# A hybrid encoder block: seven half-size products for the first half of K only, plain products for the second

## The chip, the cores and the metric

The kernel runs on one core of a Trainium2 chip. The metric is device time in microseconds (us) of one launch; the median of three runs of the kernel before is 1590.06 us (1582.69 to 1591.21). The engines are named as the profile names them: PE is TensorE (PEld its weight loads), DVE is VectorE, ACT is ScalarE, POOL is GpSimd, SP is SyncE, which issues nearly all DMAs; ACT issues some too.

## The reference

One layer on x of 1024 tokens by 2048 features, all in float32:

```python
h = rmsnorm(x, norm_w[l])
proj = jnp.einsum('bsd,de->bse', h, w_in[l])                 # 2048 -> 5632
q_a, k_a, v_a, g_a, q_r, k_r, v_r, g_r = jnp.split(proj, points, axis=-1)
attn = windowed_attention(q_a, k_a, v_a, attn_sink[l], rel_bias)      # 16 heads of 64, +-128 tokens
attn = rmsnorm(attn, attn_out_norm_w[l]) * jax.nn.silu(g_a)
ret = bidirectional_retention(rotary(q_r), rotary(k_r) * 64 ** -0.5, v_r, decay_fwd, decay_bwd)
ret = head_groupnorm(ret, ret_gn_w[l]) * jax.nn.silu(g_r)             # 8 heads, chunks of 128
mixed = jnp.concatenate([attn, ret], axis=-1)
x = x + jnp.einsum('bse,ed->bsd', mixed, w_out[l])           # 2048 -> 2048
return rmsnorm(x, final_norm_w)
```

(The reshapes into heads are left out here.)

## The kernel before

**Precision.** Every float32 operand of the large products is split into a high and a low fp32r part: ACT casts the high part (`split`, L163), POOL or DVE subtracts it to get the low part (L157). A product is then three matmuls: high by high, high by low, low by high. `wh` and `wl` are the parts of a weight tile, `hT` holds 28 rows of 128x1024: in one row the high part of a 128x512 block of activations and beside it the low part.

**Stages.** K is the 2048 features, sixteen tiles of 128.

1. Six plain units (`STD`: keys, values and queries of the attention), each 256 columns by 1024 tokens over all of K, four PSUM banks a unit. Meanwhile `combine(0)` and `combine(1)` make, for each half of K, 28 blocks of sums and differences of the normalised activations and store them in `cd`.
2. Sixteen units (`FAST`: the gates `ga` and `gr`, the retention's `qk` and `vr`), each 256 columns by 1024 tokens, twice: q = 0 to 15 is the first half of K, q = 16 to 31 the second. Each time the unit is a 2x2 by 2x2 block product done with seven half-size products instead of eight (`multiply`, L1001 to L1003; four K tiles and so 12 matmuls a product, 84 a unit). The seven weight tiles are sums and differences that `prep_sums` makes, on POOL in the first half of K and on DVE in the second, each split before use. `collect` puts the results together on ACT and DVE. The first half goes to DRAM (`yd`); the second half loads it back into the tiles `e11`, `e12`, `e2` (`partial`, L1027), adds its own, and passes the unit on: SiLU for the gates (stored in `gd`), rotation for `qk` (`rqk`), transposes for `vr` (L1106, stored in `vrd` by ACT's queue, L107).
3. The output projection: two halves of 512 tokens, four units of 512 columns each, sixteen K rows a unit (L1309 to L1311), weights split by ACT and DVE. The last unit is done bank by bank with weights that lie ready (L1335 to L1337).

**What runs between.** After every third large matmul the code calls `point()`, which advances three queues of generators: `jobs` (attention while the first half of K runs; retention while the second half does, one head pair p at a time, a step each 2.42 points), `post`, and `aux`. A retention job loads keys, queries and values (`rk`, `rq`, `vt`, L665 to L667) and starts multiplying by `vt` at its fifth step (L707). `premix` in `aux` (L845 to L847) loads an attention row `md`, its gate `gd` and the norm `rbd`, multiplies them on POOL and stores the row back to `md`; later `mixed_load` (L863) and `mixed_rows` load each row again and split it into `hT` on ACT (L878) and DVE (L160). For the first 512 tokens they do that at the very end of the second half of K and in the first output unit, in the order `ROWS`; for the last 512 tokens in the output units after it.

**Order.** Each engine works through its instructions in the order in which they stand. The order is set by where the code records them and by the generators' paces. Short-lived 128x512 tiles (`t2`) come from a ring of six: the seventh waits until the first is free. The raw weight tiles (`r`) have eight buffers, `wh` and `wl` three each, and the large products four PSUM banks (`psMa` and `psMb`, two each).

## Time and profile before

| what | us |
|---|---|
| profiled execution, device time | 1581.0 |
| its span, first to last instruction | 1579.2 |
| plain units, to 301 | 301 |
| first half of K, 301 to 730 | 429 |
| second half of K, 730 to 1195 | 465 |
| output, first 512 tokens, 1195 to 1392 | 197 |
| output, last 512 tokens, 1392 to the end | 187 |
| median of the three runs | 1590.06 |

The stage borders are the starts of the stage's first large matmul in the trace. In a group line of the profile the last fields are busy time, mean duration of one in ns, idle time of the engine just before, and what ended that idle time. A matmul's recorded duration is longer than the distance to the next one, because matmuls overlap; the distance is what counts. PEclk is the share of the TensorE clock that was granted.

### The profile page before, as it was taken

To read this page: it belongs to the slowest core of one execution; us is meant where nothing else is said; L and a number is where in the kernel's file an instruction comes from. 1 tells how busy PE (TensorE), PEld (TensorE's weight loads), DVE (VectorE), ACT (ScalarE), POOL (GpSimd) and SP (SyncE) were. 2 spreads that over 40 slices of the span, in tenths; PEclk is the share of its full clock that TensorE was granted. 3 is DMA by queue.
4 is the path that set the end of the run, shared out by engine and by line. 5 is a ranking of instruction groups with operands and counts; after the bars stand their busy time and mean duration, and the time that the engine had idled before them with its cause. 6 is when DMAs were issued, how large, how long until landed. Compare 5 with 4: busy or idle time off the path is not lost.

```text
span 1579.2 us, 21950 instructions
## 1 busy us (share of the span) xinstructions
PE 1486.1 (94%) x7250; PEld 1230.2 (78%) x7250; DVE 912.4 (58%) x1872; ACT 666.0 (42%) x1401; POOL 614.3 (39%) x481
## 2 busy tenths in 40 slices
PE   8999999999999999999998989799888989999997
PEld 6898877778888888887777777677676868878886
DVE  6565345863653664577758868659684353364323
ACT  5311135765765775775321332232343343324210
POOL 3232221356557456544653635665443200113000
PEclk9999999999999999999999999899998999999999
DMA  8888768784564564538763554684737864565403
GB/s 311 286 268 299 259 180 288 246 271 128 148 185 134 160 181 142 167 118 295 238 226 136 187 187 150 209 288 135 244 136 238 279 217 131 161 216 196 128 20 107
DMA packets 195406, 311.73 MB, mean 197 GB/s; under 512 B 29355, under 2 KB 67243, under 8 KB 194652
## 3 DMA queue, kind: packets, MB, share of 16 engines
q1 hardware_dynamic: 164828, 289.36, 56.4%
q10 hardware_dynamic: 30464, 20.98, 4.2%
q8 instruction: 57, 0.93, 0.2%
q14 instruction: 57, 0.47, 0.1%
HBM read 216.38 MB, written 93.88 MB: 196 GB/s over the span
## 4 chain that ended last, share of the span: by engine, by line
PE 50%; DMA 17%; DVE 10%; issue 9%; POOL 7%; ACT 4%; SPq 3%; POOLq 0%; ACTq 0%; DVEq 0%
POOL wl L157 4%; PE psMa L1003 4%; PE psMa L1001 4%; PE psMa L1002 4%; PE psMb L1001 3%; PE psMb L1003 3%; PE psMb L1002 3%; PE psST L574 2%; DMA t<-mpd 2%; PE psST L1310 2%; PE psMa L1310 2%; PE psST L1309 2%; DMA cd<-crow 2%; PE psST L1311 2%; DVE t L157 2%
## 5 line engine op out<-in xcount | busy, mean ns | idle before, releaser
L157 POOL TENSOR_TENSOR wl<-r,wh 128x512 fp32r<-128x512 f32 x224 | 299.4, 1340 | 328.1 <-ACT wh L163 296.6
L1001 PE MATMUL psMa<-hT,wh 128*128 128x512 f32 x512 | 209.8, 410 | 15.0 <-DVE bmv L757 6.5
L1003 PE MATMUL psMa<-hT,wl 128*128 128x512 f32 x512 | 205.0, 400 | 6.5 <-POOL wl L157 6.5
L1002 PE MATMUL psMa<-hT,wh 128*128 128x512 f32 x512 | 202.9, 396 | 0.0
L163 ACT CAST wh<-r 128x512 fp32r<-128x512 f32 x224 | 136.8, 617 | 153.4 <-PE psMa L1002 67.5
L163 ACT CAST wh<-e 128x512 fp32r<-128x512 f32 x160 | 98.2, 618 | 215.7 <-PE psMb L1311 79.5
L157 DVE TENSOR_TENSOR wl<-e,wh 128x512 fp32r<-128x512 f32 x112 | 85.6, 770 | 137.0 <-ACT wh L163 134.7
L1001 PE MATMUL psMb<-hT,wh 128*128 128x512 f32 x384 | 156.5, 408 | 3.8 <-DVE bmv L757 3.8
L1003 PE MATMUL psMb<-hT,wl 128*128 128x512 f32 x384 | 152.6, 397 | 2.9 <-POOL wl L157 2.9
L157 POOL TENSOR_TENSOR wl<-e,wh 128x512 fp32r<-128x512 f32 x48 | 72.4, 1512 | 204.6 <-ACT wh L163 192.9
L1002 PE MATMUL psMb<-hT,wh 128*128 128x512 f32 x384 | 151.2, 394 | 0.0
L1001 PEld LDWEIGHTS psMa<-hT,wh 128*128 128x128 f32 x512 | 97.9, 191 | 35.1 <-issue 11.8
L1003 PEld LDWEIGHTS psMa<-hT,wl 128*128 128x128 f32 x512 | 97.7, 191 | 34.3 <-POOL wl L157 13.3
L1002 PEld LDWEIGHTS psMa<-hT,wh 128*128 128x128 f32 x512 | 98.3, 192 | 16.0
L600 DVE CUSTOM_DVE_ANT_0 P<-psST,bias,nsink 128x384 f32<-128x384 f32 (+1 forms) x128 | 74.4, 581 | 34.3 <-PE psST L592 33.3
L604 ACT ACTIVATE P<-P,nmx 128x385 f32<-128x385 f32 (+1 forms) x128 | 75.8, 592 | 37.7 <-DVE nmx L600 36.1
L1003 PEld LDWEIGHTS psMb<-hT,wl 128*128 128x128 f32 x384 | 72.9, 190 | 22.7 <-POOL wl L157 6.5
L157 POOL TENSOR_TENSOR r<-r,r 128x512 f32<-128x512 f32 x64 | 84.7, 1334 | 3.8
L1001 PEld LDWEIGHTS psMb<-hT,wh 128*128 128x128 f32 x384 | 73.2, 191 | 16.4 <-ACT wh L163 4.3
L1002 PEld LDWEIGHTS psMb<-hT,wh 128*128 128x128 f32 x384 | 73.2, 191 | 12.1
L157 DVE TENSOR_TENSOR r<-r,r 128x512 f32<-128x512 f32 x64 | 60.1, 952 | 35.7 <-POOL wl L157 34.1
L157 POOL TENSOR_TENSOR hT<-t,hT 128x512 fp32r<-128x512 f32 x16 | 21.4, 1335 | 130.7 <-ACT hT L163 130.7
(338 smaller groups left out, 3589.0 us busy)
## 6 DMA issues: line engine op xcount, KB each, us to landing
r<-in_w_fast SPq DMA_DIRECT2D x128, 256.0 KB, 3.3
e<-in_w_out SPq DMA_DIRECT2D x112, 256.0 KB, 3.4
yd<-e SPq DMA_DIRECT2D x64, 256.0 KB, 3.1
e<-yd SPq DMA_DIRECT2D x64, 256.0 KB, 3.1
t<-in_xT SPq DMA_DIRECT2D x31, 512.0 KB, 6.3
t<-cd SPq DMA_DIRECT2D x56, 256.0 KB, 4.3
e<-in_w_in SPq DMA_DIRECT2D x48, 256.0 KB, 4.6
md<-t SPq DMA_DIRECT2D x48, 256.0 KB, 2.7
```

The lines of the kernel that those rows point to most:

```text
L157: eng.tensor_tensor(o, x, y, op)
L163: A.copy(o_hi, x)
L574: T.transpose(p[:, 128 * i : 128 * i + 128], x[:, 128 * i : 128 * i + 128], ident)
L600: V.tensor_tensor_reduce(x[:, :W], p[:, :W], bias[2 * pr + c][:, k0 : k0 + W], -1.0, nsink[:, head : head + 1], ALU.add, ALU.min, nmx[:, c ...
L604: A.activation(x[:, : W + 1], x[:, : W + 1], AF.Exp, bias=nmx[:, c : c + 1], scale=-1.0, accum_out=sums[:, c : c + 1])
L1001: T.matmul(bank, wh[:, ws], hh, start=(j == 0 and p in (0, 1, 3)), stop=False, skip_group_check=True)
L1002: T.matmul(bank, wh[:, ws], hl, start=False, stop=False, skip_group_check=True)
L1003: T.matmul(bank, wl[:, ws], hh, start=False, stop=(j == 3), skip_group_check=True)
L1309: T.matmul(p, mh, wh, start=(k == 0), stop=False)
L1310: T.matmul(p, mh, wl, start=False, stop=False)
L1311: T.matmul(p, ml, wh, start=False, stop=(k == NK - 1))
```

## The change

- `prep_sums`, `multiply` and `collect` now run for the first half of K alone (16 units of 84 matmuls). `combine` makes 28 blocks instead of 56; `normalise_rest` stores the sixteen normalised blocks of the second half of K in `xd` (8 K tiles, two token halves).
- The second half is sixteen plain units. Each has four weight tiles (`w_half`, 128x512: two K tiles by 256 columns). For each tile the four PSUM banks (two column groups by two token halves) are taken one after the other, six matmuls each (two K tiles by three parts, L1310 to L1312): 96 matmuls a unit. All sixteen units use the same four banks. The part from the first half of K is loaded at the second weight tile, and DVE adds it as it empties the bank.
- What follows a unit is now a generator in `post`: `gate_post`, `rope_post`, `value_post`. The retention is let go when `value_post` has ended, two points after its last store.
- `premix`, `mixed_load` and `mixed_rows` are gone. `mixed_row` loads a row, for attention also gate and norm, multiplies on POOL, splits into `hT` on ACT and DVE, and stores nothing. The generator `mixer` makes the rows of the first 512 tokens while the plain units run, as soon as their gate or retention is done, then those of the last 512 tokens. `ROWS` has another order.
- Paces: attention 2.62 instead of 2.65 points a step, retention 2.9 instead of 2.42, `aux` 1.1 instead of 1.3 in the output.

```diff
-ROWS = [0, 1, 2, 3, 8, 9, 10, 11, 12, 13, 4, 5, 14, 15, 6, 7]
+ROWS = [0, 1, 8, 9, 2, 3, 10, 11, 12, 13, 4, 5, 14, 15, 6, 7]
...
     def w_load(i):
         if i < n_w[0] and i not in wraw and i not in wsp:
-            r = et_("e11" if i < W_STD else ("e11", "e2", "e12", "e2", "e11", "e12", "e2")[(i - W_STD) % 7])
+            if i < W_STD:
+                r = et_("e11")
+            elif i < W_ALL:
+                r = rt(F32)
+            else:
+                r = et_(("e11", "e2", "e12", "e2", "e11", "e12", "e2")[(i - W_ALL) % 7])
             SP.dma_start(r, w_src(i))
             wraw[i] = r
...
-    pt, due, pace, adue, apace = [0], [0], [2.65], [0], [2.0]
+    pt, due, pace, adue, apace = [0], [0], [2.62], [0], [2.0]
...
+    def normalise_rest():
+        loaded = {}
+        for i in range(8 + 2):
+            if i < 8:
+                loaded[i] = t4()
+                SP.dma_start(loaded[i], a["xT"][8 + i])
+            yield
+            if i >= 2:
+                x = loaded.pop(i - 2)
+                for z in range(2):
+                    y = x[:, 512 * z : 512 * z + 512]
+                    stt(V, y, y, nw[:, 6 + i : 7 + i], rb[z], ALU.mult, ALU.mult)
+                    store(xd[2 * (i - 2) + z], y, x)
+                yield
...
+    def mixed_row(kk, hf):
         sl = slice(512 * hf, 512 * hf + 512)
-        r, g, n = t2(), t2(), t2()
+        r = t2()
         SP.dma_start(r, md[128 * kk : 128 * kk + 128, sl])
-        SP.dma_start(g, gd[128 * kk : 128 * kk + 128, sl])
-        SP.dma_start(n, rbd[:, sl])
-        for _ in range(5):
-            yield
-        tt(G, g, g, n, ALU.mult)
-        tt(G, r, r, g, ALU.mult)
-        yield
-        store(md[128 * kk : 128 * kk + 128, sl], r, r, lambda: done.add(("pre", kk, hf)))
-        yield
...
+        if kk < 8:
+            g, n = t2(), t2()
+            SP.dma_start(g, gd[128 * kk : 128 * kk + 128, sl])
+            SP.dma_start(n, rbd[:, sl])
+            for _ in range(5):
+                yield
+            tt(G, g, g, n, ALU.mult)
+            tt(G, r, r, g, ALU.mult)
+        for _ in range(3):
+            yield
+        if hf and kk >= 12:
+            omix[kk] = (rt(F32R), rt(F32R))
+        c = ew[:, kk : kk + 1]
+        A.activation(orow(kk, hf, 0), r, AF.Copy, scale=c)
+        yield
+        stt(V, orow(kk, hf, 1), r, c, orow(kk, hf, 0).bitcast(F32), ALU.mult, ALU.subtract)
+        done.add(("mix", kk, hf))
+        yield
...
-        eng = V if q >= NF else G
+        eng = G
...
+    def value_post(i, tiles):
+        yield
+        yield
+        for b, t in enumerate(tiles):
+            et, hf = b // 2, b % 2
+            p = pT()
+            for c in range(4):
+                T.transpose(p[:, 128 * c : 128 * c + 128], t[:, 128 * c : 128 * c + 128], ident)
+            o = t2()
+            A.copy(o, p)
+            store_now(vrd[i, :, 4 * hf : 4 * hf + 4, 128 * et : 128 * et + 128], o.rearrange("p (c e) -> p c e", c=4))
+            yield
+            yield
+        done.add(("vr", i))
...
+    def mixer():
+        for hf in range(2):
+            order = ROWS if hf == 0 else range(16)
+            for n in range(0, 16, 2):
+                pair = order[n : n + 2]
+                need = ("ga", pair[0] // 2) if pair[0] < 8 else ("ret", (pair[0] - 8) // 2)
+                yield ready(need)
...
+    for u, (kind, i) in enumerate(FAST):
+        if u == 2:
...
-            pace[0], apace[0] = 2.42, 2.2
+            pace[0], apace[0] = 2.9, 2.2
             for g in range(4):
                 jobs.append((retention(g), None))
...
+            aux.append((mixer(), None))
+        whole = pM()
+        tiles = []
+        for w in range(4):
+            wi = W_STD + 4 * u + w
...
+            w_load(wi + 2)
+            wh, wl = wsp.pop(wi)
+            for b in range(4):
+                et, hf = b // 2, b % 2
+                p = whole[b]
+                if w == 1:
+                    tiles.append(quarter(b))
+                    SP.dma_start(tiles[b], yd[u, b])
+                for kk in range(2):
+                    ws = slice(256 * kk + 128 * et, 256 * kk + 128 * et + 128)
+                    row = 2 * (2 * w + kk) + hf
+                    hh, hl = hT[:, row, 0:512], hT[:, row, 512:1024]
+                    last = (w, kk) == (3, 1)
+                    T.matmul(p, wh[:, ws], hh, start=(w, kk) == (0, 0), stop=False)
+                    T.matmul(p, wh[:, ws], hl, start=False, stop=False)
+                    T.matmul(p, wl[:, ws], hh, start=False, stop=last)
+                    if last:
+                        tt(V, tiles[b], p, tiles[b], ALU.add)
+                    point()
+                if b == 0:
+                    w_split(wi + 1)
...
                 if un == 0:
-                    mixed_rows()
-                    if k in (5, 6, 7, 8, 9, 10):
-                        mixed_load(ROWS[k + 5], 0)
-                    if k == 13:
-                        mixed_flush()
+                    drain(aux, ("mix", kk, 0))
+                elif un == 4:
+                    drain(aux, ("mix", kk, 1))
```

The order of the instructions shows what moves. On PE, at the border of two products in the second half before (`psMa_8627` and `psMa_8453` are banks, `hT` the activations; L680 is a transpose of the retention):

```order
L1001 MATMUL psMa_8627<-hT,wh_8673 128x512
L1002 MATMUL psMa_8627<-hT,wh_8673 128x512
L1003 MATMUL psMa_8627<-hT,wl_8674 128x512
L680 MATMUL psST_8783<-ident,rk_8647 128x128 x4
L1001 MATMUL psMa_8453<-hT,wh_8720 128x512
```

and on PE at the border of two units in the changed kernel, last weight tile of the one, first of the next:

```order
L1312 MATMUL psMb_8178<-hT,wl_8285 128x512
L1310 MATMUL psMb_8179<-hT,wh_8284 128x512
L1311 MATMUL psMb_8179<-hT,wh_8284 128x512
L1312 MATMUL psMb_8179<-hT,wl_8285 128x512
L1310 MATMUL psMb_8179<-hT,wh_8284 128x512
L1311 MATMUL psMb_8179<-hT,wh_8284 128x512
L1312 MATMUL psMb_8179<-hT,wl_8285 128x512
L1310 MATMUL psMa_8360<-hT,wh_8328 128x512
```

A weight tile now serves four banks in turn, two K tiles each, and the next unit starts at once in the bank that the unit before closed 18 matmuls earlier.

On DVE in the second half before (`r` are weight tiles of `prep_sums`, `e` the unit's four results, `t` a retention result):

```order
L157 TENSOR_TENSOR t_1964_9286<-psST_9355,t_1964_9286 128x512
L157 TENSOR_TENSOR e_1959_9259<-psMa_8903,e_1959_9259 128x512
L157 TENSOR_TENSOR r_9298<-r_9298,r_9297 128x512
L157 TENSOR_TENSOR r_9429<-r_9299,r_9298 128x512
L157 TENSOR_TENSOR r_9297<-r_9297,r_9299 128x512
L157 TENSOR_TENSOR e_1969_9302<-psMb_9372,e_1969_9302 128x512
L157 TENSOR_TENSOR e_1969_9302<-psMa_9182,e_1969_9302 128x512
```

and in the changed kernel, a value unit's four results, then the retention (`sd`, `ST`), then the first of the next unit:

```order
L159 TENSOR_TENSOR e_1729_8226<-psMa_8176,e_1729_8226 128x512
L159 TENSOR_TENSOR e_1733_8243<-psMa_8177,e_1733_8243 128x512
L159 TENSOR_TENSOR e_1734_8251<-psMb_8178,e_1734_8251 128x512
L159 TENSOR_TENSOR e_1737_8266<-psMb_8179,e_1737_8266 128x512
L159 TENSOR_TENSOR sd_8517<-psST_8512,dt_8456 128x512
L740 COPY ST_8533<-psST_8528 64x384
L162 SCALAR_TENSOR_TENSOR ST_8533<-ST_8533,cdec,psST_8528 64x128 x2
L159 TENSOR_TENSOR e_1763_8422<-psMa_8360,e_1763_8422 128x512
```

The weight sums are gone from DVE, and each result is touched once where it was touched up to twice.

On ACT in the first output unit before (`wh` casts of the output weights, L878 rows of the mixed activations, L754 and L776 the retention's last outputs):

```order
L776 ACTIVATE on_11855<-on_11855,bnt_11934,bny_11867 128x128 x4
L878 ACTIVATE hT<-t_2515_12059,ew 128x512
L878 ACTIVATE hT<-t_2520_12088,ew 128x512
L163 CAST wh_11998<-e_2486_11919 128x512
L754 COPY on_11979<-psO_11952 128x512
L163 CAST wh_12029<-e_2495_11961 128x512
L878 ACTIVATE hT<-t_2528_12123,ew 128x512
```

and in the changed kernel (L884 is the row, L799 the retention's output):

```order
L799 ACTIVATE on_11701<-on_11701,bnt_11757,bny_11713 128x128 x4
L165 CAST wh_11791<-e_2350_11740 128x512
L165 CAST wh_11809<-e_2355_11770 128x512
L884 ACTIVATE hT<-t_2371_11866,ew 128x512
L165 CAST wh_11833<-e_2359_11795 128x512
L884 ACTIVATE hT<-t_2375_11896,ew 128x512
L165 CAST wh_11851<-e_2362_11813 128x512
```

The last rows still stand between the casts of the first output unit: four of the sixteen rows of the first 512 tokens, where it was six before. The rows of the last 512 tokens follow them directly.

More of the change, by code (lines that the diff above doesn't have):

```diff
@@ L435, in load @@
             for y in range(2):
[L436 removed]
+                SP.dma_start(loaded[j][y], a["xT"][4 * y + j])
         load(0)
@@ L451, in combine @@
             for p, x, y in ((0, b11, 0), (6, b22, 1), (1, b21, 1)):
-                store(cd[ph, 4 * p + j], x, loaded[j][y])
+                store(cd[4 * p + j], x, loaded[j][y])
             def less(p, x, y):
@@ L456, in less @@
                 tt(V, c, x, y, ALU.subtract)
-                last = (lambda: done.add(("built", ph))) if (j, p) == (3, 5) else None
-                store(cd[ph, 4 * p + j], c, c, last)
+                store(cd[4 * p + j], c, c)
                 return c
@@ L952, in after @@
         yield ready(*names)
+        assert all(n in done for n in names), names
         yield from gen
@@ L1033, in take @@
         def take(b, bank):
-            o = partial(q, b)
-            if q >= NF:
-                tt(V, o, bank, o, ALU.add)
-            else:
-                A.copy(o, bank)
+            A.copy(partial(q, b), bank)
         def more(b, bank):
@@ L1463, in _layout @@
     fast = [
-        columns(*u).reshape(2, 2, 4, 128, 2, 128)[h].transpose(3, 0, 2, 1, 4).reshape(2, 2, 128, 512)
-        for h in range(2)
-        for u in FAST
+        columns(*u)[:1024].reshape(2, 4, 128, 2, 128).transpose(3, 0, 2, 1, 4).reshape(2, 2, 128, 512) for u in FAST
     ]
+    half = [columns(*u)[1024:].reshape(4, 2, 128, 256).transpose(0, 2, 1, 3).reshape(4, 128, 512) for u in FAST]
     fast = [f.reshape(4, 128, 512) for f in fast]
```

223 lines of the change are left out of this document (102 added, 121 removed).

## Prediction

> **What bounds the kernel now.** I read the page first, then the busy time by stage, then PE's waits in the stages that change. A measurement of this kernel tells about 0.5% from no change: the three runs span 0.54%.
>
> ```profile
> span 1579.2 us, 21950 instructions
> ...
> PE 1486.1 (94%) x7250; PEld 1230.2 (78%) x7250; DVE 912.4 (58%) x1872; ACT 666.0 (42%) x1401; POOL 614.3 (39%) x481
> ...
> PEclk9999999999999999999999999899998999999999
> ```
>
> PE is the bound, and almost full. The stages (columns: busy time of PE, PEld, DVE, ACT, POOL, granted clock, DMA share, GB/s) say where it is not:
>
> ```profile
> 301.00:730.00 429.00, 420.63 (x2195) 356.65 (x2195) 249.67 (x658) 285.73 (x669) 240.14 (x184) 1.00 0.56 172
> 730.00:1195.00 465.00, 417.35 (x2023) 335.44 (x2022) 333.54 (x628) 152.48 (x292) 246.08 (x196) 0.96 0.60 200
> ...
> 1195.00:1252.30 57.30, 50.73 (x221) 40.95 (x220) 24.32 (x58) 18.07 (x34) 16.00 (x13) 0.94 0.75 250
> 1252.30:1304.60 52.30, 47.69 (x194) 37.54 (x193) 24.55 (x37) 21.92 (x41) 3.07 (x2) 0.93 0.71 232
> 1304.60:1391.60 87.00, 87.00 (x385) 72.04 (x384) 30.15 (x42) 28.20 (x55) 6.67 (x5) 1.00 0.45 140
> ```
>
> The first half of K (301 to 730) is idle on PE for 8.4 us and has the full clock. The second half, with as many products, is idle for 47.6 us at a mean clock of 0.96, and DVE is busy for 333.54 us of 465 there. Output units three and four (1304.6 to 1391.6) never wait: 384 matmuls in 87.00 us give the **price of a large matmul, 0.2266 us**. Units one and two wait. The waits of PE in the second half, in us in total, times, longest:
>
> ```profile
> PE psST L707 <- DMA vt<-vrd: 12.2, 4, 3.8
> PE psMa L1003 <- POOL wl L157: 6.5, 9, 2.3
> PE psMa L1001 <- DVE bmv L757: 6.5, 1, 6.5
> PE psMa L1001 <- ACT wh L163: 4.8, 4, 2.8
> PE psST L787 <- ACT on L776: 4.2, 3, 2.8
> PE psMb L1001 <- DVE bmv L757: 3.8, 1, 3.8
> PE psMa L1001 <- DVE e L157: 2.8, 3, 1.6
> PE psMb L1003 <- POOL wl L157: 2.7, 4, 1.4
> PE psO L748 <- DVE ST L160: 1.9, 2, 1.3
> PE psO L748 <- DVE qs L157: 1.0, 2, 0.8
> PE psMa L1001 <- DVE bnt L157: 1.0, 1, 1.0
> ```
>
> They add up to 47.4 us. The clock costs on top of them 0.04 of 465 us, 18.6 us. How it falls is seen around one wait:
>
> ```profile
> 814.11 0.50 PE L1003 MATMUL psMa<-hT,wl 128*128 128x512 f32 x1 [2.33 <-POOL wl L157]
> ...
> 811.00:815.00 4.00, 1.67 (x8) 1.06 (x7) 2.07 (x2) 0.62 (x1) 3.43 (x3) 1.00 0.75 279
> 815.00:818.40 3.40, 3.40 (x10) 2.43 (x8) 0.20 (x1) 0.62 (x1) 3.24 (x3) 0.51 0.47 148
> ```
>
> After 2.33 us of waiting, the next 3.4 us run at about half the clock. So the stage holds some 66 us that are neither product nor retention, and they are all that the change can win there.
>
> **The change part by part.**
>
> *More products, certain.* The second half drops 16 x 84 = 1344 matmuls and gets 16 x 96 = 1536: 192 more, at 0.2266 us **+43.5 us** on PE. Nothing hides it.
>
> *Waits for weights and results* (POOL `wl` 9.2, ACT `wh` 4.8, DVE `e` 2.8: 16.8 us).
>
> ```profile
> L157 DVE TENSOR_TENSOR r<-r,r 128x512 f32<-128x512 f32 x61 | 58.2, 965 | 34.5 <-POOL wl L157 32.9 <-DMA t<-cd 1.2
> L157 DVE TENSOR_TENSOR e<-psMa,e 128x512 f32<-128x512 f32 x63 | 42.8, 683 | 14.0 <-PE psMa L1003 13.3
> ...
> L157 POOL TENSOR_TENSOR wl<-r,wh 128x512 fp32r<-128x512 f32 x111 | 151.2, 1367 | 154.7 <-ACT wh L163 146.0 <-PE psST L787 4.4 <-PE psMa L1003 2.6
> ```
>
> The weight sums leave DVE: 58.2 us busy and 34.5 us in which DVE stood still for POOL. Weight tiles to split fall from 112 to 64, which takes 48 x 1.367 = 65.6 us off POOL; results taken from banks fall from 112 to 64, 48 x 0.683 = 32.8 us off DVE. A tile then feeds 24 matmuls (5.4 us) where it fed 12 (2.7 us), against 1.37 us for its low part. Bounds 0 and 16.8 left; I take 4, near the first half of K, whose whole idle time is 8.4 us.
>
> *The two long waits* (`bmv`, 10.3 us). The engine named had long been done. In the 6.5 us one, ACT stood before a value unit's copy, and the weight casts stood behind it:
>
> ```profile
> 1002.15 0.59 ACT L1108 COPY t<-psST 128x512 f32<-128x512 f32 x1 [6.12 <-POOL t L157]
> ```
>
> That POOL product belongs to `premix`: it waited for loads, and held buffers of the ring that the copy needed. The product of the row stays, but its store and its second load go. Bounds 0 and 10.3; I take 3.
>
> *The values' way* (`vt`, 12.2 us).
>
> ```profile
> DMA to landing us min/median/max: 4.7/5.3/6.1
> ...
> vt<-vrd SPq DMA_DIRECT2D x4, 1024.0 KB, 5.3
> vrd<-t ACTq DMA_DIRECT2D x16, 256.0 KB, 4.0
> ```
>
> The last transposed block has to land (4.0) and be loaded with the rest (5.3) before L707. By the order of the instructions 32, 45, 34 and 45 large matmuls lie between the last value transpose and that line; in the changed kernel 45, 78, 51 and 84, since the job starts two points later and its steps are 2.9 points apart. That gives 13, 33, 17 and 39 more, 2.9 to 8.8 us, against waits of at most 3.8. Bounds 0 and 12.2; I take 1.5.
>
> *The retention's own waits* (`on` 4.2, `ST` 1.9, `qs` 1.0, `bnt` 1.0: 8.1 us). Wider steps and a freer ACT, DVE and POOL help; the chain is the same. Bounds 0 and 8.1; I take 4.
>
> *Clock.* 12.5 of 47.4 us of waits left; I let the clock's loss shrink alike, from 18.6 to 4.9. Together the stage wins 34.9 + 13.7 = **48.6 us**. The Trainium skill, "TensorE: Matmul & The Clock Gate", section "HAM oscillation — how this bites in real kernels", says that idle gaps above about 3.4 us bring the slow clock. The trace differs: 2.33 us were enough. By the page, waits that shrink below 3.4 us would win all 18.6 us and the sum would be 4.9 us lower.
>
> *Banks used again at once.* From the close of a bank to the next unit's first matmul in it lie 18 matmuls, 4.1 us, and the result needs 0.68 us on DVE. Before it on DVE stand retention steps that wait for POOL or DMA. I take 0; what it costs without that cover is a rival below.
>
> *Mixed rows.* Units one and two of the output need 2 x 192 x 0.2266 = 87.0 us and take 109.6; some 3 us are the retention's last steps. The rest is 11.1 us of waits and 57.3 x 0.06 + 52.3 x 0.07 = 7.1 us of clock:
>
> ```profile
> PE psMa L1310 <- DVE wl L157: 3.5, 2, 3.3
> PE psST L1309 <- ACT wh L163: 2.6, 2, 1.9
> PE psST L1310 <- DVE wl L157: 2.0, 3, 1.4
> PE psMa L1309 <- ACT wh L163: 1.8, 1, 1.8
> PE psMa L1309 <- DVE e L157: 1.2, 1, 1.2
> ```
>
> ACT's casts queue behind rows that wait for `md`. Four rows instead of six stand there now, but the last retention pair ends as late as before, and the rows of the last 512 tokens bring their gates, norms and 16 POOL products (16 x 1.37 = 22 us) into these units. Bounds: all 18 won, or 10 lost; I take **-6**.
>
> *Before 730 us.* `normalise_rest` spares DVE 16 subtractions, and 12 blocks fewer are loaded and split; PE hardly waits for them: **-1**.
>
> Sum, against the profiled execution: 1581.0 + 43.5 - 48.6 - 6 - 1 = 1568.9. The median of the runs lies 9.1 us above that execution, so **1578 us**, 0.8% less.
>
> **The rivals.**
>
> - *Nearly all stalls go.* For it speaks the first half of K, with attention beside it at full clock. 5 us of waits and 2 us of clock left, output -15: 1581.0 + 43.5 - 42.4 - 16.6 - 15 - 1 = 1549.5, with 9.1 us 1559. Against it: the retention's chain has waits of its own.
> - *The banks decide; slower.* DVE takes results in its order, and one instruction that waits there holds up all four. If it comes later than 4.1 us, PE stops at the unit's start; the 6.5 us wait shows such a length. Each late border costs about 2.4 us and 3.4 us at half clock, 4.1 us together. At eight of fifteen borders that is 33 us: 1611. It decides (slower by 0.5%) from five borders on. For it: DVE's busy 333.54 us. Against: 91 us of DVE's work go, and its waits for `e` were mostly for PE itself.
> - *The output's stall stays.* ACT and POOL meet the rows of the last 512 tokens in the first two units: +8 instead of -6, 1592, no change.
> - *Micro-idling at bank changes.* Four banks in turn, with a gap at each change, and the clock falls to a mean of 0.90 in a stage of some 460 us: 46 - 5 = 41 us more, 1619. Against it stands a plain unit of today, which changes the bank every third matmul:
>
> ```profile
> 146.10:189.70 43.60, 43.60 (x194) 36.08 (x193) 21.41 (x28) 6.63 (x11) 9.71 (x7) 1.00 0.79 274
> ```
>
> The same page of the Trainium skill, section "A second HAM failure mode: psum-queue depth-cycling", describes that failure. By it the change would lose; the row above, with no idle time at clock 1.00, is why I give it little.
>
> **How the numbers follow.** Forecast 0.50 (its own range 1568 to 1592), nearly all stalls gone 0.20, banks 0.16, output's stall 0.11, micro-idling 0.03. Faster by over 0.5% means below 1582: 0.31 of the forecast's half and all of the second case, 0.51. Slower means above 1598: the banks, the micro-idling and 0.03 of tails, 0.22. Between them 0.27. The range runs from below the case of no stalls to short of eight late borders: 1556 to 1605.
>
> **What would show it.** Right: 1536 large matmuls in a second half of about 460 us (465 + 43.5 - 48.6), clock 0.98 or more; no `vt` wait above 1 us; POOL `wl` under 4 us; DVE under 260 us busy there. Wrong: waits of each unit's first matmul for DVE's `e` (banks); ACT waits for `md` or POOL `t` before the casts of output unit one (rows); a second half above 480 us with PE's waits spread as before, which would say that the retention and the queues, not the seven products, make the stalls.

## The result, and the profile after

The changed kernel takes **1547.92 us** (median of 4 runs, 1546.61 to 1550.44), beside 1586.91 us for the kernel before (4 runs, 1582.69 to 1591.21): ratio 0.9756, 95% interval 0.9721 to 0.9791. The forecast was 1578, its range 1556 to 1605. The direction was right; the gain is some three times the one forecast, and the time lies below the range. One later run of the kernel before took 3148.77 us, beside 1576 to 1590 for the twelve others of its group, and the ratios below leave it out.

The profiled execution of the changed kernel took 1548.5 us. Its page:

```profile
span 1546.7 us, 21769 instructions
...
PE 1501.8 (97%) x7442; PEld 1259.3 (81%) x7442; DVE 782.9 (51%) x1732; ACT 634.0 (41%) x1341; POOL 549.3 (36%) x433
...
PEclk9999999999999999999999999999999999999999
...
PE 78%; DMA 9%; DVE 4%; issue 3%; POOL 3%; ACT 2%; SPq 1%; POOLq 0%; ACTq 0%; DVEq 0%
```

PE has 192 matmuls more (7442 for 7250), is busy for 97% of a shorter span, and the granted clock is 0.9 or more in every slice, where two slices of the kernel before were below. The chain that ended last is now PE's own work for 78% (50% before). DVE, ACT and POOL together lost 227 us of busy time. Here are the same stages as in the prediction's table (first half of K, second half, output unit one, unit two, units three and four; columns: length, busy time of PE, PEld, DVE, ACT, POOL, granted clock, DMA share, GB/s):

```profile
297.60:737.30 439.70, 424.96 (x2195) 360.75 (x2194) 250.12 (x655) 286.75 (x671) 245.91 (x187) 0.99 0.55 170
737.30:1175.00 437.70, 434.41 (x2213) 362.68 (x2212) 216.02 (x507) 120.06 (x230) 167.05 (x138) 1.00 0.55 178
1175.00:1225.90 50.90, 49.22 (x222) 40.05 (x221) 22.78 (x57) 17.77 (x33) 10.47 (x8) 0.97 0.72 233
1225.90:1272.70 46.80, 44.80 (x194) 35.84 (x193) 20.20 (x28) 15.73 (x32) 16.89 (x12) 1.00 0.67 214
1272.70:1360.20 87.50, 87.39 (x385) 71.88 (x384) 37.36 (x50) 33.10 (x63) 9.77 (x7) 1.00 0.55 169
```

By stage, after minus before: up to the first half of K -3.4 us (it starts at 297.6 instead of 301.0), first half **+10.7**, second half **-27.3** although it holds 192 large matmuls more, output units one and two **-11.9**, units three and four +0.5, and the rest -1.1. The sum is the -32.5 us by which the span got shorter. What PE waits for in the whole run (in us in total, times, longest):

```profile
...
PE psO L582 <- ACT PTh L604: 5.8, 4, 2.3
PE psO L583 <- DVE PTl L159: 4.5, 7, 2.1
PE psMa L1007 <- DVE e L159: 4.1, 1, 4.1
PE psMa L1310 <- DVE e L159: 3.3, 3, 2.3
PE psMa L1364 <- DVE wl L159: 2.5, 3, 1.5
...
PE psST L1364 <- DVE wl L159: 2.0, 3, 1.3
PE psMa L1363 <- ACT wh L165: 1.3, 1, 1.3
```

L1310 is the plain product of the second half. Of that stage's 47.4 us of waits, 3.3 are left, each at a unit's first matmul into a bank, behind DVE's result from that bank. No wait for `vt`, `wl` or `wh` remains there. The first two rows (but for 1.2 us) and L1007 are the first half of K, where attention runs; L1363 and L1364 are the output.

### The profile page after: what moved, and what is told of

Read it like the earlier page. It is cut to its first block, busy times and chain, and to the rows that moved or that the text cites. A ratio compares the mean times of both kernels' runs of the same rounds, so it can differ in the third digit from the quotient of the medians.

```text
span 1546.7 us, 21769 instructions
## 1 busy us (share of the span) xinstructions
PE 1501.8 (97%) x7442; PEld 1259.3 (81%) x7442; DVE 782.9 (51%) x1732; ACT 634.0 (41%) x1341; POOL 549.3 (36%) x433
## 4 chain that ended last, share of the span: by engine, by line
PE 78%; DMA 9%; DVE 4%; issue 3%; POOL 3%; ACT 2%; SPq 1%; POOLq 0%; ACTq 0%; DVEq 0%
PE psMa L1310 4%; PE psMb L1310 4%; PE psMa L1312 4%; PE psMa L1311 4%; PE psMb L1311 3%; PE psMb L1312 3%; PE psMa L1007 3%; PE psMa L1008 3%; PE psMa L1009 3%; DMA t<-mpd 2%; PE psMb L1009 2%; PE psMb L1007 2%; PE psMb L1008 2%; PE psST L597 2%; PE psMa L1364 2%
## 5 line engine op out<-in xcount | busy, mean ns | idle before, releaser
L159 POOL TENSOR_TENSOR wl<-r,wh 128x512 fp32r<-128x512 f32 x176 | 233.6, 1330 | 369.4 <-ACT wh L165 344.7
L165 ACT CAST wh<-r 128x512 fp32r<-128x512 f32 x176 | 108.2, 617 | 184.1 <-PE psMb L1311 120.5
L159 DVE TENSOR_TENSOR wl<-e,wh 128x512 fp32r<-128x512 f32 x112 | 88.9, 801 | 133.9 <-ACT wh L165 130.8
L1310 PE MATMUL psMa<-hT,wh 128*128 128x512 f32 x256 | 105.2, 411 | 3.3 <-DVE e L159 3.3
L1007 PE MATMUL psMa<-hT,wh 128*128 128x512 f32 x256 | 102.1, 399 | 4.1 <-DVE e L159 4.1
L1310 PE MATMUL psMb<-hT,wh 128*128 128x512 f32 x256 | 104.5, 408 | 0.0
L1009 PE MATMUL psMa<-hT,wl 128*128 128x512 f32 x256 | 100.8, 394 | 0.0
L1008 PE MATMUL psMa<-hT,wh 128*128 128x512 f32 x256 | 100.7, 393 | 0.0
L1312 PE MATMUL psMa<-hT,wl 128*128 128x512 f32 x256 | 100.5, 393 | 0.0
L1311 PE MATMUL psMa<-hT,wh 128*128 128x512 f32 x256 | 100.4, 392 | 0.0
L1312 PE MATMUL psMb<-hT,wl 128*128 128x512 f32 x256 | 100.0, 391 | 0.0
L1311 PE MATMUL psMb<-hT,wh 128*128 128x512 f32 x256 | 99.9, 390 | 0.0
L1007 PE MATMUL psMb<-hT,wh 128*128 128x512 f32 x192 | 76.2, 397 | 0.0
L1009 PE MATMUL psMb<-hT,wl 128*128 128x512 f32 x192 | 75.6, 394 | 0.3 <-POOL wl L159 0.3
L1008 PE MATMUL psMb<-hT,wh 128*128 128x512 f32 x192 | 75.4, 393 | 0.0
L159 DVE TENSOR_TENSOR PTl<-psST,PTh 128x384 fp32r<-128x384 f32 (+1 forms) x128 | 66.5, 519 | 11.3 <-ACT PTh L604 10.8
L159 POOL TENSOR_TENSOR t<-t,t 128x512 f32<-128x512 f32 x32 | 43.4, 1358 | 74.9 <-DMA t<-rbd 42.7
```

Of the source, the lines that this page charges most:

```text
L159: eng.tensor_tensor(o, x, y, op)
L165: A.copy(o_hi, x)
L1007: T.matmul(bank, wh[:, ws], hh, start=(j == 0 and p in (0, 1, 3)), stop=False, skip_group_check=True)
L1008: T.matmul(bank, wh[:, ws], hl, start=False, stop=False, skip_group_check=True)
L1009: T.matmul(bank, wl[:, ws], hh, start=False, stop=(j == 3), skip_group_check=True)
L1310: T.matmul(p, wh[:, ws], hh, start=(w, kk) == (0, 0), stop=False)
```

## The experiments

All ratios are to the kernel before, run on the same chip beside each kernel. Its median there was 1581 to 1585 us. Stage lengths come from the profiled execution of each kernel, with borders at the first large matmul of a stage.

**The parts of the helpers' load, taken out of the kernel before.** First the weight sums of the second half alone:

```diff
-        eng = V if q >= NF else G
+        if q >= NF:
+            if part == 0:
+                sums[q] = raws[q, 1]
+            return
+        eng = G
```

> The kernel before without the weight sums on DVE in the second half of K (64 operations of 0.965 us left out, so the second half's products are of the wrong weights). Theory L with the sums as the main load: the 17 us of waits for wl, wh and e in the second half fall below 6, with their share of the clock the kernel is 15 to 25 us faster than before (1562 to 1572 us). Theory S or theory P (the rows' first pass, premix, blocks POOL, ACT and the ring): waits stay above 38 of 47 us, less than 8 us gained.

Measured: 1552.68 us (1551.62 to 1556.22), ratio 0.9819 [0.9793, 0.9844]. The second half, and PE's wait for the values there:

```profile
731.90:1165.80 433.90, 406.26 (x2022) 330.65 (x2021) 284.22 (x567) 152.89 (x292) 240.86 (x196) 0.98 0.64 213
...
PE psST L707 <- DMA vt<-vrd: 5.4, 3, 2.9
```

31.1 us shorter with 49 us of DVE's work gone, waits 47.4 to 27.2 us, clock 0.96 to 0.98. The wait for `vt`, of which no weight sum is an operand, fell from 12.2 to 5.4 us. The output does not change (57.3 and 53.4 us for its first two units).

Then the work that made the mixed rows early (three loads, two POOL products and a store for each row of attention):

```diff
-        r, g, n = t2(), t2(), t2()
-        SP.dma_start(r, md[128 * kk : 128 * kk + 128, sl])
...
-        store(md[128 * kk : 128 * kk + 128, sl], r, r, lambda: done.add(("pre", kk, hf)))
+        done.add(("pre", kk, hf))
         yield
```

> The kernel before without premix: the attention rows are taken without gate and norm, so three loads, two POOL products and one store of each of the 16 half rows are left out. Theory P: the two long waits of PE (10.3 us) and part of those for wl go, second half 15 us or more shorter, and the first two output units 5 us or more shorter; kernel 20 us or more faster than before (below 1567 us). Theory L with the sums, or theory S: second half less than 6 us shorter.

Measured: 1547.85 us (1546.05 to 1549.88), ratio 0.9788 [0.976, 0.9817]. The second half and the first two units of the output:

```profile
729.50:1176.20 446.70, 409.77 (x2022) 329.93 (x2021) 333.85 (x631) 153.90 (x294) 219.50 (x176) 0.98 0.58 189
1176.20:1223.20 47.00, 47.00 (x222) 38.93 (x221) 24.23 (x60) 20.75 (x37) 3.34 (x3) 1.00 0.67 222
1223.20:1270.20 47.00, 44.95 (x194) 35.85 (x193) 20.59 (x32) 18.50 (x35) 0.00 (x0) 1.00 0.56 174
...
PE psMb L992 <- DVE bmv L757: 4.2, 1, 4.2
```

18.3 us go from the second half, though DVE is as busy as before, and 15.6 from the output's first two units, where PE then never stops in unit one. So the early rows' work was the output's stall; which part of it (loads, products or store) this run does not separate. The two waits for `bmv`, which the prediction put down to this work, are not gone: 4.2 us (the last row) and 1.5 us stay of 10.3.

Both at once:

> The kernel before without the second half's weight sums and without premix (both left out as in the two runs that left out one of them; the results are of wrong weights and ungated rows). Alone they made the second half 31.0 and 18.1 us shorter and the kernel 28.7 and 33.5 us faster. If both are loads that add up on queues with no room: together the second half is 42 us or more shorter (below 423 us) and the kernel 55 us or more faster (below 1529 us). If each of them takes away the same stalls: together hardly more than the better one, 35 to 42 us faster.

Measured: 1516.96 us (1516.82 to 1518.34), ratio 0.9595 [0.9555, 0.9635].

```profile
730.90:1150.00 419.10, 402.23 (x2021) 328.81 (x2020) 280.27 (x569) 154.24 (x292) 215.63 (x176) 0.98 0.60 198
```

The second half is 45.9 us shorter than before. The two savings add in time: 28.7 us and 33.5 us alone, 66 together by the medians of their own comparisons (1581.37 and 1583.10 before); in the second half alone they add a little short, 45.9 for 31.1 and 18.3. None of that work is on PE. Of the two only the sums belong to the seven products; the rows' work has to be done somewhere, and the changed kernel does it without the store and reload, with 20 of the rows' 32 POOL products after the second half's end (12 before).

**The same room filled again, in the changed kernel.** At each weight tile one DVE operation on the raw tile (its maximum with itself) is added:

```diff
+            if wi + 1 < W_ALL:
+                rw = wraw[wi + 1]
+                tt(V, rw, rw, rw, ALU.max)
```

> The changed kernel with one idle operation more on DVE for each weight tile of the second half of K (the raw tile's maximum with itself, before its split; four a unit, 64 in all, as many as the sums that the change took off DVE; some 0.97 us each, 62 us). Theory L: the stalls were DVE's load, so they come back in good part: waits in the second half 15 us or more (3.3 now), 1560 us and up. If what counts is the spacing, the wider weight tiles or the rows instead: waits under 7 us, within 5 us of the changed kernel (1543 to 1553 us).

Measured: 1576.53 us (1573.59 to 1585.44, 10 runs), ratio 0.9954 [0.9927, 0.9981]. The second half, its main wait, and the group of added operations (busy, mean ns, then the idle time before them and what ended it):

```profile
736.60:1200.30 463.70, 442.91 (x2213) 368.20 (x2212) 265.60 (x566) 119.52 (x230) 168.63 (x138) 0.97 0.52 169
...
PE psMa L1313 <- DVE e L159: 17.5, 5, 6.1
...
L159 DVE TENSOR_TENSOR r<-r 128x512 f32<-128x512 f32 x63 | 54.3, 862 | 97.8 <-DMA r<-in_w_half 96.6 <-ACT on L777 0.7
```

26.0 us come back in that stage, all of it as waits for results from banks and the slow clock behind them. The third row limits what this shows: the added operations held DVE not only for 54.3 us of work but for 97.8 us in which they stood at its head and waited for the tile's load, with bank results behind them. The busy time alone was not priced. The weight sums of the kernel before stood too, but for less and nearly all of it behind POOL (34.5 us, in the prediction's row).

With the same on POOL as well (the tile added to itself, so that the products of the second half come out doubled):

> The same with one idle operation on POOL as well for each of these tiles (the raw tile added to itself, so the second half's products come out doubled; 64 of 1.34 us, 86 us), which brings POOL back to its former load. Theory L with both engines: waits in the second half 25 us or more and 1570 us and up. If the freed room is not what counts: within 8 us of the changed kernel (1540 to 1556 us).

Measured: 1601.62 us (1599.75 to 1604.32), ratio 1.0103 [1.0074, 1.0132].

```profile
737.80:1227.80 490.00, 451.54 (x2213) 370.80 (x2212) 270.30 (x566) 119.46 (x230) 233.81 (x199) 0.97 0.50 159
...
PE psMa L1314 <- DVE e L159: 23.9, 7, 7.7
```

The second half is 52.3 us longer than in the changed kernel, and the kernel is slower than the one before. With its helpers held up in this way, the plain product is a loss.

**The retention's spacing.** In the changed kernel back to a step each 2.42 points, in the kernel before on to 2.9:

```diff
-            pace[0], apace[0] = 2.9, 2.2
+            pace[0], apace[0] = 2.42, 2.2
```

> The changed kernel with the retention's step back at 2.42 points instead of 2.9. Its second half of K takes 437.7 us with 3.3 us of waits. Theory S (spacing: the wider steps and the later start took the retention's waits away): the waits on vt, on and ST come back, 8 to 15 us, with some clock lost, so the second half takes 448 us or more and the kernel is 10 us or more slower than the changed one (1558 us and up). Theory L (load: the work taken off DVE, POOL and ACT took the waits away) : under 4 us more waits, the kernel within 5 us of the changed one (1543 to 1553 us); the retention ends earlier, which may win a little in the first output unit.

> The kernel before with the retention's step at 2.9 points instead of 2.42, all else as it was. Theory S: in the second half the waits on vt, on, ST and qs (19.3 of 47.4 us) fall below 8 us and the stage is 12 us or more shorter; the retention then ends about 14 rows into the first output unit, where it is forced to an end, so that unit loses some of it. Theory L: those waits fall by less than half, the stage stays above 457 us, the kernel is not faster than before.

Measured: the changed kernel at 2.42 takes 1566.35 us (1556.55 to 1568.93), ratio 0.989 [0.985, 0.9929]. In its profiled execution (1556.55, the fastest of the four):

```profile
732.70:1182.80 450.10, 439.94 (x2241) 366.20 (x2240) 221.97 (x538) 122.82 (x238) 170.30 (x140) 0.99 0.53 174
...
PE psMb L1310 <- DVE e L159: 5.8, 2, 4.2
PE psST L730 <- DMA vt<-vrd: 0.9, 2, 0.7
```

The time is what theory S expected, its waits are not. The wait for `vt` does not return. What returns is DVE's lateness at banks: `e` 9.0 us (5.8, and 3.2 at `psMa`) where the changed kernel has 3.3. The profiled execution is 9.8 us below the median of the four, so the trace does not show all that 2.42 costs. The kernel before at 2.9 takes 1562.49 us (1559.93 to 1569.53), ratio 0.9862 [0.9826, 0.9898]. The second half and output unit one, and waits of the seven products:

```profile
730.30:1170.20 439.90, 398.95 (x1929) 322.98 (x1928) 313.23 (x570) 147.37 (x276) 241.09 (x189) 0.97 0.64 207
1170.20:1240.70 70.50, 63.47 (x313) 51.16 (x312) 45.71 (x115) 24.71 (x48) 23.00 (x18) 0.95 0.63 207
...
PE psMa L1001 <- DVE e L157: 9.2, 6, 3.6
PE psMa L1003 <- POOL wl L157: 8.6, 7, 2.9
PE psMb L1003 <- POOL wl L157: 7.0, 7, 1.5
```

One number in the kernel before was worth 1.4%, and none of the product's change is needed for it. Of the 25.1 us by which the second half got shorter, some 10 only moved: 92 retention matmuls, which start 0.11 us apart in the trace, now stand in output unit one, and it got 13.2 us longer. The retention's own waits in the stage fell from 20.3 to 7.5 us and those for `bmv` from 10.3 to none, though the rows are still made early. Those for weights and results (`wl`, `wh`, `e`) rose from 16.8 to 32.9. In all, 47.4 us became 40.4; most of the waiting only moved. At 3.3 in the changed kernel:

> The changed kernel with the retention's step at 3.3 points. From 2.42 to 2.9 points PE's waits for DVE's results in the second half fell from 10.0 to 3.3 us. If DVE's crowding at the banks is what is left: under 2 us of waits in the second half, but the retention ends some 14 points later, where the first output unit needs its rows, and up to 8 us come back there: 1545 to 1556 us. If 2.9 is still too dense: 1544 us or less.

Measured: 1555.52 us (1550.15 to 1563.26), ratio 0.9841 [0.9789, 0.9893]. The second half is 431.0 us with 68 retention matmuls fewer, and output unit one 66.9 us (50.9 in the changed kernel) with these 68 more. PE's wait for `e` in the second half is 4.0 us, not below the 3.3 of 2.9 points. By medians and by ratios it is 0.5 to 0.9% worse than at 2.9, at the edge of what the intervals tell apart; 3.3 is no improvement.

**The order of the banks.** In the changed kernel all four banks are served for one K tile before the next K tile, so that a bank closes 9 matmuls before the next unit's first one in it, not 18:

```diff
-            for b in range(4):
-                et, hf = b // 2, b % 2
-                p = whole[b]
...
-                for kk in range(2):
+            for kk in range(2):
+                for b in range(4):
+                    et, hf = b // 2, b % 2
+                    p = whole[b]
```

> The changed kernel with the four banks taken for each K tile in turn, not for a pair of K tiles: a bank is used again 9 matmuls (2.0 us) after it was closed instead of 18 (4.1 us). If the bank order matters (the rival in which DVE's results come late): each border at which DVE is busy for over 2 us stops PE; at half of the fifteen borders and 2 us each with some clock 20 us or more, 1568 us and up, with PE waiting for DVE e at the first matmul of units. If DVE has room enough: under 6 us, 1546 to 1554 us.

Measured: 1566.98 us (1564.52 to 1568.88), ratio 0.9904 [0.9878, 0.993].

```profile
737.90:1193.30 455.40, 438.32 (x2214) 364.74 (x2212) 214.28 (x515) 118.51 (x229) 165.64 (x138) 0.98 0.52 171
...
PE psMa L1310 <- DVE e L159: 13.3, 5, 6.0
```

Half the room costs 17.7 us in that stage, with PE waiting for `e` five times, the longest 6.0 us. The rival of the banks had its mechanism right: 18 matmuls of room (4.1 us) leave 3.3 us of such waits in the changed kernel, 9 leave 13.3.

**The way of the mixed rows.** In the changed kernel each attention row is stored after its two products and loaded again:

```diff
             tt(G, r, r, g, ALU.mult)
+            yield
+            SP.dma_start(md[128 * kk : 128 * kk + 128, sl], r)
+            yield
+            r = t2()
+            SP.dma_start(r, md[128 * kk : 128 * kk + 128, sl])
+            yield
+            yield
```

> The changed kernel with the attention rows stored to DRAM after POOL's products and loaded again before the split, as before the change (one more store, one more load and one more buffer of the ring for each of 16 half rows). Theory P in its narrow form (the round trip through the ring of six buffers and SP's queue made stalls): 6 us or more slower, waits in the second half or in output units one and two up by 4 us or more. If only the amount of work on DVE and POOL counts: within 4 us of the changed kernel (1544 to 1552 us).

Measured: 1574.36 us (1569.61 to 1577.9, 10 runs), ratio 0.9944 [0.992, 0.9967]. Second half, output units one, two, and three with four:

```profile
738.70:1176.30 437.60, 434.24 (x2213) 361.46 (x2212) 213.71 (x505) 117.39 (x228) 167.30 (x138) 1.00 0.57 184
1176.30:1230.20 53.90, 49.37 (x220) 40.12 (x221) 25.35 (x58) 19.35 (x35) 11.24 (x8) 0.97 0.68 227
1230.20:1285.60 55.40, 46.43 (x193) 36.83 (x191) 16.32 (x22) 14.02 (x29) 11.80 (x8) 0.97 0.66 215
1285.60:1387.70 102.10, 94.88 (x384) 74.69 (x385) 42.35 (x57) 34.75 (x66) 15.63 (x11) 0.95 0.57 181
...
PE psMa L1370 <- ACT wh L165: 8.0, 2, 4.7
...
ACT hT L891 <- DMA t<-md: 68.6, 14, 10.9
```

The second half is untouched; units one to four take 26.2 us more (211.4 for 185.2), with PE waiting for the output's weight casts as in the rows that the prediction quoted of the kernel before. ACT stands 68.6 us in these units for rows from `md` (L891), with such casts behind it; in the changed kernel that is 4.2 us, and 33.1 us for POOL's products of the rows. Put back at the rows' new place, the store and reload cost more than twice what the change gains in the output. The edit also gives each attention row four more generator steps, so the rows come later; what the lateness alone costs was not tried.

**The first half of K.** It lost 10.7 us, which nothing in the prediction spoke of. Around its largest wait in the changed kernel:

```profile
730.34 0.69 DVE L159 TENSOR_TENSOR t<-t,t 128x512 f32<-128x512 f32 x1 [2.99 <-DMA t<-mpd]
...
732.15 0.68 DVE L159 TENSOR_TENSOR e<-psMa,e 128x512 f32<-128x512 f32 x1
732.89 0.50 PE L1007 MATMUL psMa<-hT,wh 128*128 128x512 f32 x1 [4.05 <-DVE e L159]
...
733.20:738.40 5.20, 5.20 (x17) 4.08 (x16) 1.32 (x2) 1.68 (x3) 4.68 (x5) 0.67 0.86 279
```

DVE stood for a load of the attention sum with a bank's result behind it; PE waited 4.05 us, and the next 5.2 us ran at 0.67 of the clock. The wait is no accident of one execution: the six other kernels made from the changed one without touching this load have it too, 2.5 to 4.7 us, and their first half takes 437.2 to 441.3 us. An experiment gives that load three steps more time:

```diff
-                for _ in range(4):
+                for _ in range(7):
```

> The changed kernel with seven points of lead instead of four between the load of an attention sum's halves and DVE's addition. In the changed kernel's first half of K, DVE stood 2.99 us before such an addition with a bank's result behind it, and PE lost 4.05 us and then 5 us of clock at the stage's end. If that one queue is the cause of the first half's loss (439.8 us against 429.1 before): the stage is 6 us or more shorter and the kernel 1542 us or less. If the loss is spread over the attention's own waits: within 3 us of the changed kernel.

Measured: 1547.52 us (1544.59 to 1549.6), ratio 0.9759 [0.973, 0.9788]: no change.

```profile
297.20:730.10 432.90, 421.74 (x2196) 358.06 (x2195) 249.30 (x654) 285.64 (x670) 241.44 (x184) 1.00 0.55 171
730.10:1174.30 444.20, 435.83 (x2214) 363.32 (x2213) 214.69 (x507) 120.44 (x233) 170.36 (x140) 0.99 0.54 177
...
PE psMa L1310 <- DVE e L159: 7.3, 3, 6.4
```

The first half wins 6.8 us, as the reading says, and the second half loses 6.5: the wait at the border of the third and fourth unit, 2.27 us in the changed kernel, is 6.4 us here. The other 4 us of the first half's loss were not tried.

**The seven products kept, with the other two improvements.** The kernel before, with the mixed rows made without the store and reload, where the output needs them, and the retention at 2.9:

```diff
-            drain(aux if kk < 8 else jobs, ("pre", kk, hf) if kk < 8 else ("ret", (kk - 8) // 2))
...
+        if kk < 8:
+            g, n = t2(), t2()
+            SP.dma_start(g, gd[128 * kk : 128 * kk + 128, sl])
+            SP.dma_start(n, rbd[:, sl])
...
+            if stage == 1 and kk < 8:
+                tt(G, g, g, n, ALU.mult)
+                tt(G, r, r, g, ALU.mult)
...
-            pace[0], apace[0] = 2.42, 2.2
+            pace[0], apace[0] = 2.9, 2.2
```

> The kernel before with all seven products kept, but the mixed rows made where the output needs them (gate and norm loaded and multiplied beside the row, no store and no second load: the former work ahead of it, its two POOL products, stores and reloads leave the second half) and the retention's pace at 2.9 instead of 2.42. Nothing is left out. It has the 192 matmuls fewer (43.5 us) and keeps the weight sums on DVE. Theory (the helpers' load in the second half is what costs, and most of it was the rows made early and the crowded retention): from 1562 with the pace alone, the stage loses some 15 us more (18.1 were measured for the rows without the pace), the first output units 3: about 1545, range 1538 to 1555, level with or below the changed kernel's 1548. Rival (the seven products need the room that only their removal gives: sums, bank results and weight casts crowd DVE anyhow): the waits for weights and results stay, second half above 435 us, 1556 or more. Second rival (the POOL products and three loads per row now stand in the output units of a kernel whose rows come late there): second half near 425, but units one to four lose 15 us: 1560.

Measured: 1557.29 us (1554.52 to 1563.58, 6 runs), ratio 0.9837 [0.9804, 0.987]. Second half, output unit one, and waits:

```profile
732.60:1157.00 424.40, 394.47 (x1929) 320.91 (x1928) 305.78 (x563) 147.59 (x275) 228.16 (x181) 0.97 0.62 200
1157.00:1231.60 74.60, 63.69 (x313) 51.08 (x312) 44.61 (x124) 25.27 (x49) 17.31 (x13) 0.93 0.52 171
...
PE psMa L996 <- POOL wl L157: 9.4, 7, 4.3
PE psMa L994 <- DVE e L157: 6.6, 3, 3.6
```

The second half came out at the 425 us that the theory and the second rival expected, and the waits for `wl` and `e` stay, as the first rival had it (14 and 8 of the stage's 30 us). Output unit one takes 7 us more than the theory said. Units one to four together take 211.2 us beside 196.6 in the kernel before, the loss that the second rival named; but 9.1 of these 14.6 us come with the pace alone (205.7 us in the kernel before at 2.9), so some 5.5 are left for the late rows.

Some 70% of the change's gain (27 us of 36 to 39) can be had with all seven products kept. In the second half the seven products are about level with the plain one: 424.4 us and some 10 for the 92 retention matmuls that moved out, beside 437.7. So waits and slow clock there use up nearly all of the 43.5 us that they save. The changed kernel's lead over this one lies in output units one to four (185.2 us for 211.2). Whether it belongs to the plain product is not shown. At 2.9 points a step the retention does not fit into this kernel's second half, which has 448 points where the changed kernel's has 512 (a point after every third large matmul), and its end falls into output unit one; a pace between 2.42 and 2.9 with the late rows was not tried. No kernel that does all of the work is clearly faster than the changed one.

## Why the prediction was wrong, step by step

The miss is 30.1 us. Against the terms of the sum, in profiled executions:

| term | predicted | measured | miss |
|---|---|---|---|
| 192 more matmuls | +43.5 | +43.5 (43.8 by units three and four, 87.5 us for 384) | about 0 |
| second half's stalls | -48.6 | -70.8 (465.0 + 43.5 - 437.7) | -22.2 |
| output units one and two | -6 | -11.9 | -5.9 |
| before 730 us | -1 | +7.3 (-3.4 + 10.7) | +8.3 |
| later output | 0 | -0.6 | -0.6 |
| median above the profiled execution | +9.1 | -0.6 (1547.92 against 1548.5) | -9.7 |

- **Right: the price of the products.** A large matmul still takes 0.228 us where PE never waits, and the stalls pay for it. But the 66 us of waits and clock that the prediction called all that the change could win in the stage were not all: 70.8 were won.
- **Wrong, the step that failed: what is left of the stage's waits.** The prediction went group by group and left 4 of 16.8, 3 of 10.3, 1.5 of 12.2 and 4 of 8.1 us, 12.5 in all; 3.3 are left, and none of them in those groups but `e`. With the clock, whose loss was made to shrink alike, that is 9.2 + 4.9 = 14.1 of the 22.2 us. Each group was discounted by itself, as if the delays were independent. They are not: taking out the sums alone more than halved the wait for `vt`, taking out sums and early rows left 16.4 of 47.4 us, spread over most groups, and the wider steps alone moved waits from the retention to weights and results. The rival "nearly all stalls go" had this right (5 us of waits, 2 us of clock) and was given 0.20; its time of 1559 was too high by the last row of the table. That its sum without that row, 1549.5, lies so near the profiled 1548.5 is luck: the stage won 11.8 us more than it said, the output and the time before 730 us 11.4 less.
- **Clock: right in its direction, short in its amount.** That the loss shrinks with the waits was right: 18.6 us to almost none (granted clock 1.00), where 4.9 were left.
- **A part that was not counted.** Waits and clock explain 44.1 + 18.6 = 62.7 of the 70.8 us. A large matmul's record is 0.39 to 0.41 us long and the next starts 0.227 us after this one's start, so a wait that the trace shows begins some 0.16 us after PE's slot was free. The 34 waits quoted of the kernel before became 3; 31 x 0.16 gives 5 us. This is worked out from rows and was not tried. About 3 us stay open; the rounding of the clock column alone (0.005 of 465 us) is 2.3.
- **`vt`: right about the wait, wrong about why spacing pays.** No such wait is left, but the wider steps are not needed for it in the changed kernel: at 2.42 it is 0.9 us. In the kernel before they did shorten it, from 12.2 to 4.7 us. How much the later start, the plain units and the freer helpers each do to it was not separated. What returns at 2.42 is DVE's lateness at banks, so that is what the wider steps pay for, as far as the trace shows it.
- **The two long waits for `bmv`: gone, but not shown to be for the reason given.** None is left where 3 us were. Without any early rows 5.7 of the 10.3 us stay in the kernel before; at 2.9 points a step, with the early rows still made, none does. So leaving out `premix` took away 4.6 us of them, and the wider steps alone take all.
- **Mixed rows: sign right, size half.** The prediction weighed fewer late rows against rows that bring their gates into the output. What decided, by the run that puts it back, is the store and reload, which the prediction named only for the two long `bmv` waits; with the four steps more that it takes, it costs 26.2 us.
- **Before 730 us: wrong sign.** DVE's stand on `mpd` ahead of a bank result is the same mechanism as in the second half, in a stage that the change was thought to leave alone. The attention's pace went from 2.65 to 2.62 and the order of the work around it moved; which of these put that load late was not tried.
- **The offset.** 9.1 us were added because three runs had a median above the profiled execution. Seven to thirteen later runs of the kernel before gave medians of 1581 to 1585 us: the profiled 1581.0 lies up to 3.6 us below them, not 9.1, and three runs that span 8.5 us do not carry such a term.
- **Of the rivals:** the banks did not decide, but are real (17.7 us at half the room). The output's stall shrank. The micro-idling at bank changes did not show: four banks in turn ran for 437.7 us at a clock of 1.00; the 0.90 in that rival was assumed, and no run shows it.
- **The signs to look for** were all met on the side of right: clock 1.00, no `vt` and no POOL `wl` wait, DVE 216 us busy in the second half (under 260). Only the stage's length, 437.7 for about 460, was beyond them. Of the signs of wrong one appeared, in small: units' first matmuls into a bank behind `e`, 3.3 us.

## What to carry to other kernels

An algorithm that saves the bound engine work is priced by what its extra helpers' work makes that engine wait, clock included, and not by whether the helpers look half idle: here DVE at 72% and POOL at 53% of a stage, the early rows' work included, were enough to cost PE more than the 43.5 us that the seven products saved it, and without the early rows still about as much. Look at what stands at the head of each helper's queue (a load, another helper) with a bank's result behind it, and count the matmuls between a bank's close and its next use. Where one helper's delay sits behind another's, forecast the waits as gone or not gone together.

## What the runs showed of the hardware that was not expected

A short wait is dear. In the changed kernel's second half DVE stood 5.03 us for a load of the retention with two bank results behind it; of that PE lost 2.27 us by waiting, and the 3.6 us after it ran at 0.54 of the clock, 1.7 us more:

```profile
807.35 0.68 DVE L159 TENSOR_TENSOR qs<-rq,qd 64x512 f32<-64x512 f32 x1 [5.03 <-DMA rq<-rqk]
807.96 1.27 DVE L159 TENSOR_TENSOR e<-psMa,e 128x512 f32<-128x512 f32 x2
808.78 0.76 PE L1310 MATMUL psMa<-hT,wh 128*128 128x512 f32 x1 [2.27 <-DVE e L159]
...
808.80:812.40 3.60, 3.60 (x9) 2.84 (x10) 1.63 (x3) 0.00 (x0) 2.88 (x3) 0.54 0.21 57
```

The Trainium skill, page "TensorE: Matmul & The Clock Gate", section "HAM oscillation — how this bites in real kernels", puts the slow clock behind gaps of more than about 3.4 us. The row above differs, as the kernel before did (2.33 us); the 4.05 us wait in the first half of K, with 5.2 us at 0.67 behind it, agrees.

The runs of one kernel spread unlike those of another, for no reason found here: in four runs each, the changed kernel over 0.25%, with DVE and POOL held up, for all its waits, over 0.29%, and at 2.42 points a step over 0.8%.
